# Gate and up products of a split-precision decoder turned token-major, with their results transposed for the down products and two of eight weight blocks used twice from one buffer

## The chip, the cores and the metric

The kernel runs on one core of a Trainium2 chip. A core has five engines that run side by side, each with its own queue of instructions: TensorE (PE; its weight loads are shown as PEld), VectorE (DVE), ScalarE (ACT), GpSimd (POOL) and SyncE (SP), which here issues the transfers between the chip's main memory and the on-chip memory SBUF. TensorE writes its sums into PSUM, eight banks of 128 partitions x 512 float32. The metric is the device time of one execution in microseconds (us); lower is better.

## The reference

Two layers; each is a half-step feed-forward, a mixing block (three kinds of attention, gated) and a second half-step feed-forward, with an RMS norm before and after each of them. Everything is float32. What the change touches are the four feed-forwards.

```python
D_MODEL = 1024; SEQ = 512; DEPTH = 2
D_FF = ((8 * D_MODEL // 3 + 127) // 128) * 128        # 2816

def _swiglu(t, w_gate, w_up, w_down):
    return (jax.nn.silu(t @ w_gate) * (t @ w_up)) @ w_down

for l in range(DEPTH):
    f = _swiglu(_rmsnorm(h, ffn1_pre_g[l]), ffn1_w_gate[l], ffn1_w_up[l], ffn1_w_down[l])
    h = h + 0.5 * _rmsnorm(f, ffn1_post_g[l])
    u = _rmsnorm(h, mix_pre_g[l])
    ...
    f = _swiglu(_rmsnorm(h, ffn2_pre_g[l]), ffn2_w_gate[l], ffn2_w_up[l], ffn2_w_down[l])
    h = h + 0.5 * _rmsnorm(f, ffn2_post_g[l])
```

## The kernel before

**Precision.** A float32 operand is split into a high part, rounded to TensorE's fp32r type (a cast on ScalarE, line 179), and a low part, the rest (a subtraction on VectorE, line 180). A product takes three matmuls (`mm3`, lines 205 to 207): high x high, high x low, low x high.

**Tiling of a feed-forward.** Tokens are 512, model features 1024, hidden features 2816. Of the hidden features 2048 are taken in two chunks (`ci` = 0, 1) of 1024; the last 768 are done plainly, with 512-wide matmuls. A chunk's gate product, up product and down product are each a 2 x 2 block product done with seven block products instead of eight (Strassen's scheme in Winograd's form): the seven are numbered n = 0 to 6 and run in the order `ORDER = (0, 2, 1, 3, 4, 5, 6)` in gate and up groups; `TO[n]` says which quarter of the result (half of the tokens, half of the chunk's features) is finished with product n; `SUM[n]` says which of three pairs of PSUM banks it adds into. Products 0, 3, 5 and 6 add on into one pair, and the result is read out on the way after 3, 5 and 6.

**Gate and up groups** (`feature_product`, line 727). The left factor is a sum of blocks of the normalized input, with features on the partitions, split into a high and a low tile: 4 slices (k) of 128 x 256 tokens. The first four products of a feed-forward's first gate group have these sums made beside them by VectorE and ScalarE (`sums`, line 680; tiles `x..`, `uh..`, `ul..`); later groups use them again. The right factor is a sum or difference of blocks of the weights, 4 slices of 128 x 512. A matmul holds 128 x 128 of the weights stationary and streams 256 tokens, so that the result has features on partitions. For a gate group the result goes through silu into tiles `s` (tag `f`, four buffers); for an up group VectorE multiplies it by the gate tile and writes it to `hr` (`hidden_rows`), for n = 4 and 5 after adding the part read out earlier (lines 764, 766, 771). Down products take their left factor from `hr` (`first_factor`, line 789: sums and splits), keep 128 x 128 of it stationary and stream 512 columns of weights (`product`, line 809).

**Weights.** A block of a product comes as two units (`BlockUnit`, line 274), each 2 slices of 128 x 512 float32 (512 KB), fetched by one transfer into a buffer with tag `raw` (2 buffers) or `o` (8, of which 4 are for this while the hidden state is parked in main memory). Per group the blocks fetched are those in `BLOCKS`, one for each of the seven products, and an eighth at n = 2 into a tile that is kept (`Keep`: names `tg`, `tu`, `bt`), in which VectorE builds differences (line 315). Names: `raw_ga`, `wh_ga`, `wl_ga` are the raw, high and low tiles of gate weights of the feed-forward `a` of a layer; `u` stands for up, `d` for down, `c` for the second feed-forward.

**Order of work.** A planner (`Queue`, line 338) holds the jobs in the order of `PLAN` (line 1576): seven gate products of chunk 0, seven up products, the same for chunk 1, then down products between plain gate and up work. When a job starts, its units are split and those of the next jobs (`AHEAD = 4` units) too; each time a unit's raw buffer is given back, `fetch_ahead` (line 399) issues the next transfers as far as the buffer counts in `RINGS` allow. A scheduler then sets the order of the instructions on each engine by their dependencies and priorities, and can place a few matmuls of the next group ahead of the last product of a group. On each engine instructions run in that order.

Of the kernel before, what the change touches and what calls it, by code (L numbers as in the profile page):

```python
# [13 lines left out]
ALU = mybir.AluOpType  # L14
# [3 lines left out]
P = 128  # L18
# [4 lines left out]
def kernel(  # L23
# [38 lines left out]
    nc = tc.nc  # L62
    _, S, D = x.shape
# [3 lines left out]
    ND = D // P  # L67
# [7 lines left out]
    FC = 8  # L75
# [12 lines left out]
    ident = cst.tile([P, P], F32, name="ident")  # L88
# [20 lines left out]
    def pbank(tag, name):  # L109
        return ps.tile([P, S], F32, tag=tag, bufs=4, name=name)  # L110
# [92 lines left out]
    def mm3(pt, lh, ll, rh, rl, start, stop, free=False):  # L203

        nc.tensor.matmul(pt, lh, rh, start=start, stop=False, skip_group_check=free)  # L205
        nc.tensor.matmul(pt, lh, rl, start=False, stop=False, skip_group_check=free)  # L206
        nc.tensor.matmul(pt, ll, rh, start=False, stop=stop, skip_group_check=free)  # L207
# [21 lines left out]
    PE_US = 1 / 2370.0  # L229


    class Unit:
# [26 lines left out]
        def loaded(self):  # L259
            self.raw = None  # L260
            Q.took(self.place, -1)
            Q.fetch_ahead()
# [11 lines left out]
    class BlockUnit(Unit):  # L274
# [9 lines left out]
        def __init__(self, n, src, rows, k0, nk, ncol, keep, name, place="raw"):  # L284
            super().__init__(src, k0, nk, 0, ncol, name)
            self.n, self.rows, self.keep, self.fetched, self.place = n, rows, keep, False, place

        def waits(self):
            return not self.fetched
# [6 lines left out]
        def fetch(self):  # L296
            if self.fetched:
                return
            self.fetched = True
            if self.n == 2:  # L300
                tc.keep_in_program_order(self.block(self.keep.get(self.k0), (0, 1)))
            Q.took(self.place, 1)
            self.raw = stile([P, self.nk, self.ncol], self.place, "raw_" + self.name, F32)
            self.block(self.raw[:], self.BLOCKS[self.n])

        def load(self):
            if self.h is not None:
# [282 lines left out]
    def ffn(l, src, wg, wu, wd, dst, name, spare, parked, plan, aside=None):  # L590
# [133 lines left out]
                return [block(i, j, part) for part in range(2)]  # L724
            return st["u", n]

        def feature_product(ci, up, n, uns):

            nm = f"{name}{'gu'[up]}_{ci}_{n}"
            if n in (0, 1, 2):  # L730
                st["c", n] = [pbank("z" if n == 0 else "mm", f"pw{nm}_{e}") for e in range(2)]
            if n == 1:
                for e in range(2):
                    nc.scalar.copy(st["c", 1][e][:], st["c", 0][e][:])
            if n == 0:
                if not up:
                    st["s", ci] = {}
            pts = st["c", SUM[n]]
            h, l = in_product(n)
            opens, ends = n in (0, 2), n in (1, 4, 6)  # L740
            for un in uns:
                for k in range(un.nk):
                    kk = un.k0 + k
                    for f in range(FC // 2):
                        c = slice(f * P, (f + 1) * P)
                        o = pts[f // 2][:, (f % 2) * S // 2:(f % 2 + 1) * S // 2]
                        mm3(o, un.h[:, k, c], un.l[:, k, c], h[:, kk], l[:, kk], opens and kk == 0 and f % 2 == 0,
                            ends and kk == FC // 2 - 1, free=True)
                        yield 3 * (S // 2) * PE_US
            if n == 0:  # L750
                return
            q = TO[n]
            g = st["s", ci]
            if not up and q not in g:
                g[q] = stile([P, FC // 2, S // 2], "f", f"s{name}_{ci}_{q[0]}{q[1]}", F32)[:]
            g = g[q]
            r = hidden_rows(2 * ci + q[1])[:, :, HALVES[q[0]]] if up else g
            for e in range(2):
                p = pts[e][:].rearrange("p (f q) -> p f q", f=2)
                re, ge = r[:, 2 * e:2 * e + 2], g[:, 2 * e:2 * e + 2]  # L760
                if n in (2, 3):
                    nc.scalar.copy(re, p)
                elif n in (4, 5):
                    nc.vector.tensor_tensor(re, re, p, ALU.add)
                elif up:
                    nc.vector.tensor_tensor(re, p, ge, ALU.mult)
                else:
                    nc.scalar.activation(re, p, AF.Silu)
            if n in (4, 5):
                if up:  # L770
                    nc.vector.tensor_tensor(r, r, g, ALU.mult)
                else:
                    nc.scalar.activation(r, r, AF.Silu)

        def feature_products(ci, up):

            w, nm = (wu if up else wg)[l, :, ci * FC * P:(ci + 1) * FC * P], f"{'gu'[up]}{name}_{ci}"
            keep = Keep(lambda k0: stile([P, 2, S], "o", f"t{nm}_{k0}", F32)[:])
            places = itertools.cycle(("raw", "o", "o"))
            for n in ORDER:  # L780
                uns = [BlockUnit(n, w, ND // 2, k, 2, S, keep, f"{nm}_{n}_{k}", next(places)) for k in range(0, ND // 2, 2)]
                run = lambda n=n, uns=uns: feature_product(ci, up, n, uns)
                early = ci == 0 and not up and n in ORDER[:4]
                yield uns, (lambda run=run: beside(run(), itertools.islice(st["some"], 1), 2)) if early else run

# [23 lines left out]
        def product(ci, n, uns):  # L809
            if n == 0 and ci == 0:  # L810
                RINGS["o"] = 2
                dst.begin()
            if n < 6:
                first_factor(ci, n + 1)
            if n in (0, 1, 2):
                st["b", SUM[n]] = [pbank("z", f"pd{name}_{ci}_{n}_{e}") for e in range(2)]
            pts = st["b", SUM[n]]
            if n == 1 and ci:
                for e in range(2):
                    nc.scalar.copy(pts[e][:], dst.fs[e][:, HF[0]])  # L820
            h, l = st["a", ci, n]
            opens, ends = n in (0, 2) or (n == 1 and not ci), n in (1, 4, 6)
            for un in uns:
                for k in range(un.nk):
                    kk = un.k0 + k
                    for e in range(2):
                        c = slice(e * P, (e + 1) * P)
                        mm3(pts[e][:], h[:, kk, c], l[:, kk, c], un.h[:, k], un.l[:, k], opens and kk == 0,
                            ends and kk == FC // 2 - 1, free=True)
                        yield 3 * S * PE_US  # L830
            if n == 0:
                return
            i, hf = TO[n]
            for e in range(2):
                f = dst.fs[2 * i + e][:, HF[hf]]
                if n == 1:
                    nc.scalar.copy(f, st["b", 0][e][:])
                    nc.vector.tensor_tensor(f, f, pts[e][:], ALU.add)
                elif ci == 0 and n in (2, 3, 6):
                    nc.scalar.copy(f, pts[e][:])  # L840
                else:
                    nc.vector.tensor_tensor(f, f, pts[e][:], ALU.add)

        def products(ci):

            keep = Keep(lambda k0: stile([P, 2, S], "o", f"bt{name}_{ci}_{k0}", F32)[:])
            w = wd[l, ci * FC * P:(ci + 1) * FC * P]
            for n in range(7):
                uns = [BlockUnit(n, w, FC // 2, k, 2, S, keep, f"d{name}_{ci}_{n}_{k}", ("raw", "o")[k // 2])
                       for k in range(0, FC // 2, 2)]  # L850
                yield uns, (lambda n=n, uns=uns: product(ci, n, uns))

        marks, made = {}, {}
# [16 lines left out]
        def queue(what):  # L870
            kind, n = what[0], what[1]
            if kind in "gu":
                if n not in made:
                    made[n] = plain(n)
                ms = (what[2],) if what[-1] in (0, 1) and len(what) == 3 else range(2)
                uns = made[n][kind == "u"]
                run = (lambda: gates(n, uns, ms)) if kind == "g" else (lambda: ups(n, uns, ms))
                Q.add(uns if ms[0] == 0 else [], run)
            elif kind == "a":
                Q.add([], lambda: iter(first_factor(n, 0) or ()))  # L880
            elif kind == "m":
                if name == "a0":
                    Q.add([], mem_stats)
            else:
                if what not in made:
                    made[what] = products(n) if kind == "d" else feature_products(n, kind == "U")
                for one in made[what]:
                    Q.add(*one)
                    break
# [746 lines left out]
```

## Time and profile before

| | |
|---|---|
| median of 3 runs | 2410.04 us (2409.96 to 2410.2) |
| profiled execution, whole | 2413.01 us |
| its span, first to last instruction | 2411.3 us |
| TensorE busy | 2383.9 us |
| VectorE busy | 1865.6 us |
| ScalarE busy | 1357.8 us |
| moved by transfers | 372.10 MB, mean 154 GB/s |

In profile rows, an instruction group has its line in the kernel, engine, operation, output <- inputs, shape and count. Rows of the timeline begin with the start and the duration in us. Matmuls are pipelined, so their durations overlap: the distance between two starts says what one costs in a stream, and the duration how long it is under way. In a row of waits stand who waited for what, and then the total in us, the times and the longest. In a row of the kind "270/272/273" stand the shortest, median and longest duration in ns, then the first and the last start.

### The profile page before, as it was taken

To read this page: it belongs to the slowest core of one execution; us is meant where nothing else is said; L and a number is where in the kernel's file an instruction comes from. 1 tells how busy PE (TensorE), PEld (TensorE's weight loads), DVE (VectorE), ACT (ScalarE), POOL (GpSimd) and SP (SyncE) were. 2 spreads that over 40 slices of the span, in tenths; PEclk is the share of its full clock that TensorE was granted. 3 is DMA by queue.
4 is the path that set the end of the run, shared out by engine and by line. 5 is a ranking of instruction groups with operands and counts; after the bars stand their busy time and mean duration, and the time that the engine had idled before them with its cause. 6 is when DMAs were issued, how large, how long until landed. Compare 5 with 4: busy or idle time off the path is not lost.

```text
span 2411.3 us, 36506 instructions
## 1 busy us (share of the span) xinstructions
PE 2383.9 (99%) x14407; PEld 2129.1 (88%) x14407; DVE 1865.6 (77%) x2462; ACT 1357.8 (56%) x2137; POOL 81.5 (3%) x134
## 2 busy tenths in 40 slices
PE   9999999999999999999999999999999999999998
PEld 8998889888888899988899988889888888999887
DVE  8878877678776688788698788766778766887885
ACT  6555565567655555455554554656676655545554
POOL 1000000000110000000000000000001100000000
PEclk9999999999999999999999999999999999999999
DMA  6765454222223466655557655542222234676544
GB/s 236 229 198 185 157 193 140 79 71 71 82 68 114 149 217 201 209 174 176 186 183 227 202 184 174 189 118 71 71 88 74 63 127 150 200 230 198 176 156 157
DMA packets 249344, 372.10 MB, mean 154 GB/s; under 512 B 11450, under 2 KB 126162, under 8 KB 249172
## 3 DMA queue, kind: packets, MB, share of 16 engines
q1 hardware_dynamic: 249076, 369.74, 47.9%
q8 instruction: 113, 1.85, 0.3%
q14 instruction: 59, 0.48, 0.1%
q0 software_dynamic: 96, 0.03, 0.0%
HBM read 357.14 MB, written 12.58 MB: 153 GB/s over the span
## 4 chain that ended last, share of the span: by engine, by line
PE 84%; DVE 7%; DMA 4%; ACT 3%; issue 2%; SPq 0%; DVEq 0%; ACTq 0%
PE pg L205 3%; PE pg L206 3%; PE pg L207 3%; PE pda L206 3%; PE pda L207 3%; PE pda L205 3%; PE pdc L206 2%; PE pdc L207 2%; PE pdc L205 2%; PE pb L207 1%; PE pb L206 1%; PE pb L205 1%; DMA raw_wo<-in_w_out_dram 1%; PE pwc1g L205 1%; PE pwc0g L205 1%
## 5 line engine op out<-in xcount | busy, mean ns | idle before, releaser
L205 PE MATMUL pg<-us_a,wh_wg 128*128 128x512 f32 x384 | 151.7, 395 | 0.0
L206 PE MATMUL pg<-us_a,wh_wg 128*128 128x512 f32 x384 | 150.6, 392 | 0.0
L207 PE MATMUL pg<-us_a,wl_wg 128*128 128x512 f32 x384 | 150.5, 392 | 0.0
L206 PE MATMUL pda<-wl_da,aha 128*128 128x512 f32 x224 | 87.5, 391 | 0.7 <-DVE wl_da L180 0.7
L206 PE MATMUL pdc<-wl_dc,ahc 128*128 128x512 f32 x224 | 87.5, 391 | 0.5 <-DVE wl_dc L180 0.5
L207 PE MATMUL pdc<-wh_dc,alc 128*128 128x512 f32 x224 | 87.2, 389 | 0.0
L207 PE MATMUL pda<-wh_da,ala 128*128 128x512 f32 x224 | 87.2, 389 | 0.0
L180 DVE TENSOR_TENSOR wl_dc<-raw_dc,wh_dc 128x1024 fp32r<-128x1024 f32 x50 | 61.1, 1222 | 33.2 <-ACT wh_dc L179 32.6
L205 PE MATMUL pda<-wh_da,aha 128*128 128x512 f32 x224 | 86.5, 389 | 0.0
L205 PE MATMUL pdc<-wh_dc,ahc 128*128 128x512 f32 x224 | 86.5, 389 | 0.0
L207 PEld LDWEIGHTS pg<-us_a,wl_wg 128*128 128x128 f32 x384 | 72.7, 189 | 15.5
L205 PEld LDWEIGHTS pg<-us_a,wh_wg 128*128 128x128 f32 x384 | 73.0, 190 | 14.6
L206 PEld LDWEIGHTS pg<-us_a,wh_wg 128*128 128x128 f32 x384 | 72.9, 190 | 14.6
L179 ACT CAST wh_dc<-raw_dc 128x1024 fp32r<-128x1024 f32 x50 | 52.7, 1053 | 57.6 <-PE pdc L207 17.7
L183 DVE SCALAR_TENSOR_TENSOR wl_wg<-raw_wg,wh_wg 128x1024 fp32r<-128x1024 f32 x48 | 58.5, 1223 | 33.9 <-ACT wh_wg L182 33.6
L180 DVE TENSOR_TENSOR wl_da<-raw_da,wh_da 128x1024 fp32r<-128x1024 f32 x50 | 61.1, 1222 | 24.4 <-ACT wh_da L179 23.9
L179 ACT CAST wh_da<-raw_da 128x1024 fp32r<-128x1024 f32 x50 | 52.6, 1053 | 44.4 <-PE pda L207 17.6
L179 ACT CAST wh_uc<-raw_uc 128x1024 fp32r<-128x1024 f32 x44 | 46.2, 1049 | 51.0 <-PE pwc0u L206 12.6
L180 DVE TENSOR_TENSOR wl_uc<-raw_uc,wh_uc 128x1024 fp32r<-128x1024 f32 x44 | 53.8, 1222 | 25.6 <-ACT wh_uc L179 24.9
L179 ACT CAST wh_ua<-raw_ua 128x1024 fp32r<-128x1024 f32 x44 | 46.0, 1049 | 41.6 <-PE pwa1u L206 12.6
L180 DVE TENSOR_TENSOR wl_ua<-raw_ua,wh_ua 128x1024 fp32r<-128x1024 f32 x44 | 53.6, 1221 | 20.0 <-ACT wh_ua L179 19.3
L182 ACT ACTIVATE wh_wg<-raw_wg 128x1024 fp32r<-128x1024 f32 x48 | 50.8, 1061 | 26.6 <-PE pv L1044 13.5
(640 smaller groups left out, 8933.2 us busy)
## 6 DMA issues: line engine op xcount, KB each, us to landing
raw_da<-in_ffn_w_down_dram SPq DMA_DIRECT2D x74, 512.0 KB, 4.7
raw_dc<-in_ffn_w_down_dram SPq DMA_DIRECT2D x74, 512.0 KB, 4.8
raw_ga<-in_ffn_w_gate_dram SPq DMA_DIRECT2D x68, 512.0 KB, 4.5
raw_ua<-in_ffn_w_up_dram SPq DMA_DIRECT2D x68, 512.0 KB, 4.3
raw_gc<-in_ffn_w_gate_dram SPq DMA_DIRECT2D x68, 512.0 KB, 4.2
raw_uc<-in_ffn_w_up_dram SPq DMA_DIRECT2D x68, 512.0 KB, 4.3
raw_wg<-in_w_gate_dram SPq DMA_DIRECT2D x48, 512.0 KB, 3.5
raw_wo<-in_w_out_dram SPq DMA_DIRECT2D x24, 512.0 KB, 3.7
```

The costliest lines, as they stand in the source:

```text
L179: both = [nc.scalar.copy(h_ap, src)]
L180: make = lambda: nc.vector.tensor_tensor(l_ap, src, h_ap.bitcast(F32), ALU.subtract)
L182: both = [nc.scalar.activation(h_ap, src, AF.Copy, scale=scale)]
L183: make = lambda: nc.vector.scalar_tensor_tensor(l_ap, src, scale, h_ap.bitcast(F32), ALU.mult, ALU.subtract)
L205: nc.tensor.matmul(pt, lh, rh, start=start, stop=False, skip_group_check=free)
L206: nc.tensor.matmul(pt, lh, rl, start=False, stop=False, skip_group_check=free)
L207: nc.tensor.matmul(pt, ll, rh, start=False, stop=stop, skip_group_check=free)
```

## The change

Gate and up products swap the roles of their factors: 128 x 128 of the activations are stationary, and 512 weight columns stream, so that the result has tokens on partitions. The product of silu(gate) and up is written over the gate tile; `turn` then transposes each finished quarter on TensorE, eight 128 x 128 transposes into two PSUM banks, and copies them on ScalarE into `hr`, where the down products find features on partitions as before. `turn` is called in the next product, after its third slice of four; for the last up product of chunk 1 this is the first down product.

Where two products that follow each other use the same block (n = 0 and 2, n = 3 and 4 in gate and up groups; n = 3 and 4 in down groups), the second takes over the buffer of the first (`inherits`) and issues no transfer; the buffer is given back after the second.

```diff
@@ class BlockUnit
             self.n, self.rows, self.keep, self.fetched, self.place = n, rows, keep, False, place
+            self.heir = None
+
+        def inherits(self, un):
+            un.heir, self.place = self, None
@@ fetch
             self.fetched = True
             if self.n == 2:
                 tc.keep_in_program_order(self.block(self.keep.get(self.k0), (0, 1)))
+            if self.place is None:
+                return
             Q.took(self.place, 1)
             self.raw = stile([P, self.nk, self.ncol], self.place, "raw_" + self.name, F32)
             self.block(self.raw[:], self.BLOCKS[self.n])
+
+        def loaded(self):
+            if self.heir is None:
+                super().loaded()
+            else:
+                self.heir.raw, self.heir.place, self.raw = self.raw, self.place, None
@@ feature_product, now token_product
-                    for f in range(FC // 2):
-                        c = slice(f * P, (f + 1) * P)
-                        o = pts[f // 2][:, (f % 2) * S // 2:(f % 2 + 1) * S // 2]
-                        mm3(o, un.h[:, k, c], un.l[:, k, c], h[:, kk], l[:, kk], opens and kk == 0 and f % 2 == 0,
-                            ends and kk == FC // 2 - 1, free=True)
-                        yield 3 * (S // 2) * PE_US
+                    for e in range(2):
+                        c = slice(e * P, (e + 1) * P)
+                        mm3(pts[e][:], h[:, kk, c], l[:, kk, c], un.h[:, k], un.l[:, k], opens and kk == 0,
+                            ends and kk == ND // 2 - 1, free=True)
+                        yield 3 * S * PE_US
+                    if kk == ND // 2 - 2:
+                        yield from turn("z")
...
                 elif up:
-                    nc.vector.tensor_tensor(re, p, ge, ALU.mult)
+                    nc.vector.tensor_tensor(ge, p, ge, ALU.mult)
...
             if n in (4, 5):
                 if up:
-                    nc.vector.tensor_tensor(r, r, g, ALU.mult)
+                    nc.vector.tensor_tensor(g, r, g, ALU.mult)
                 else:
                     nc.scalar.activation(r, r, AF.Silu)
-
-        def feature_products(ci, up):
+            if up and n in (1, 4, 5, 6):
+                st["turn"] = (f"{nm}", g, r)
+
+        def turn(tag):
+
+            nm, g, r = st.pop("turn", (None, None, None))
+            if nm is None:
+                return
+            g = g.rearrange("p f q -> p (f q)")
+            for b in range(2):
+                pt = pbank(tag, f"ht{nm}_{b}")
+                for f in range(2):
+                    for e in range(2):
+                        nc.tensor.transpose(pt[:, (2 * f + e) * P:(2 * f + e + 1) * P],
+                                            g[:, e * S + (2 * b + f) * P:][:, :P], ident[:])
+                nc.scalar.copy(r[:, 2 * b:2 * b + 2], pt[:].rearrange("p (f q) -> p f q", f=2))
+                yield 0.4
+
+        def token_products(ci, up):
...
-            places = itertools.cycle(("raw", "o", "o"))
+            places, had = itertools.cycle(("raw", "o", "o")), {}
             for n in ORDER:
-                uns = [BlockUnit(n, w, ND // 2, k, 2, S, keep, f"{nm}_{n}_{k}", next(places)) for k in range(0, ND // 2, 2)]
-                run = lambda n=n, uns=uns: feature_product(ci, up, n, uns)
+                uns = [BlockUnit(n, w, ND // 2, k, 2, S, keep, f"{nm}_{n}_{k}", n in (2, 4) or next(places))
+                       for k in range(0, ND // 2, 2)]
+                if n in (2, 4):
+                    for un, of in zip(uns, had[n - 2 + (n == 4)]):
+                        un.inherits(of)
+                had[n] = uns
+                run = lambda n=n, uns=uns: token_product(ci, up, n, uns)
@@ product (down)
                         yield 3 * S * PE_US
+                    if kk == FC // 2 - 2:
+                        yield from turn("mm")
@@ products (down)
+                if n == 4:
+                    for un, of in zip(uns, had):
+                        un.inherits(of)
+                had = uns
```

More of the change, by code (lines that the diff above doesn't have):

```diff
@@ L725, in in_product, with token_product @@
             return st["u", n]
-        def feature_product(ci, up, n, uns):
+        def token_product(ci, up, n, uns):
             nm = f"{name}{'gu'[up]}_{ci}_{n}"
@@ L885, in queue @@
                 if what not in made:
-                    made[what] = products(n) if kind == "d" else feature_products(n, kind == "U")
+                    made[what] = products(n) if kind == "d" else token_products(n, kind == "U")
                 for one in made[what]:
```

## The prediction

> **What bounds the kernel now.** I read the page's busy times first, then the same times by stage, then what the matmul engine waited for.
>
> ```profile
> span 2411.3 us, 36506 instructions
> PE 2383.9 (99%) x14407; PEld 2129.1 (88%) x14407; DVE 1865.6 (77%) x2462; ACT 1357.8 (56%) x2137; POOL 81.5 (3%) x134
> ...
> 38.80:82.00 43.20, 43.09 (x358) 42.75 (x357) 41.83 (x43) 28.09 (x35) 3.99 (x5) 1.00 0.65 209
> 82.00:122.50 40.50, 39.93 (x331) 39.53 (x330) 33.56 (x39) 23.89 (x29) 0.00 (x0) 1.00 0.70 213
> 122.50:163.00 40.50, 40.42 (x337) 40.22 (x336) 29.41 (x28) 22.58 (x27) 0.00 (x0) 1.00 0.67 209
> 163.00:204.00 41.00, 41.00 (x336) 40.59 (x336) 33.52 (x32) 21.53 (x25) 0.00 (x0) 1.00 0.39 116
> ```
>
> The last four rows are the gate, up, gate, up groups of the first feed-forward (length, then PE, PEld, DVE, ACT, POOL, clock, DMA share, GB/s). TensorE is busy all through at the full granted clock, so each group is paid in matmul time. The one engine near it is VectorE, above all in the first gate group (41.83 of 43.20 us). DMA is at 0.4 to 0.7. TensorE's waits in the whole run that lie in the stages touched:
>
> ```profile
> PE pdc L206 <- DVE wl_dc L180: 1.3, 2, 0.8
> PE pwa1g L207 <- DVE wl_ga L180: 1.2, 1, 1.2
> ...
> PE pda L206 <- DVE wl_da L180: 0.7, 1, 0.7
> PE pwc0g L207 <- DVE wl_gc L180: 0.7, 1, 0.7
> ...
> PE pwa0g L207 <- DVE wl_ga L180: 0.4, 1, 0.4
> ...
> PE pwc0u L205 <- DVE hrc L764: 0.2, 1, 0.2
> PE pwa0u L205 <- DVE hra L764: 0.2, 1, 0.2
> PE pwa1u L205 <- DVE hra L764: 0.2, 1, 0.2
> PE pwc1u L205 <- DVE hrc L764: 0.2, 1, 0.2
> ```
>
> That is 3.1 us in gate and up groups and 2.0 us in down products. Almost nothing can be won by ending waits; what counts is the time that the matmuls themselves take.
>
> **Part 1: half as many matmuls, each twice as wide.** Four feed-forwards x two chunks x gate and up are 16 groups of seven products. A product falls from 4 k x 4 f x 3 = 48 matmuls of 256 columns to 4 k x 2 e x 3 = 24 of 512: 5,376 become 2,688, with as many weight loads fewer. Their durations (0.28 and 0.39 us below) overlap, so the price is the distance between starts, in stretches without a wait:
>
> ```profile
> 180.10 0.28 PE L207 MATMUL pwa0u<-uha,wl_ua 128*128 128x256 f32 x1
> ...
> 189.82 0.28 PE L207 MATMUL pwa0u<-uha,wl_ua 128*128 128x256 f32 x1
> ...
> 228.90 0.39 PE L207 MATMUL pda<-wh_da,ala 128*128 128x512 f32 x1
> ...
> 235.70 0.39 PE L207 MATMUL pga<-us_x,wl_ga 128*128 128x512 f32 x1
> ```
>
> The first pair lies 81 matmuls apart: 9.72/81 = 120.0 ns. The second lies 30 apart: 6.80/30 = 226.7 ns. The down products (pda) already have the new shape: a 128x128 piece of activations stationary, 512 weight columns moving. Two narrow ones cost 240.0, one wide one 226.7: 13.3 ns saved, x 2,688 = **-35.8 us**, 0.32 us a product.
>
> The Trainium skill, page "TensorE: Matmul & The Clock Gate", section "Back-to-back issue gap", gives a gap of N/2.4 + 2.5 ns for a matmul of N columns at full clock, so only 2.5 ns per instruction. By it the saving would be an estimated 6.7 us and the whole change slower. The rows speak against it here: 120.0 and 226.7 fit 256 and 512 columns at 2.4 per ns plus 13.3 ns each.
>
> **Part 2: transposes.** The result now has tokens on partitions, and the down products want features there. Each up group transposes four tiles (`turn`), each with 8 transposes and 2 ScalarE copies: 32 turns, 256 transposes, 64 copies. The same operation, eight at a time between wide matmuls, stands in the trace:
>
> ```profile
> 1554.29 0.39 PE L207 MATMUL pda<-wh_da,hida 128*128 128x512 f32 x1
> 1554.53 1.03 PE L565 MATMUL uta<-ident,fa 128*128 128x128 f32 x8
> ...
> 1555.63 0.40 PE L206 MATMUL pda<-wl_da,hida 128*128 128x512 f32 x1
> ...
> L565 PE MATMUL uta<-ident,fa x64: 270/272/273, 356.6 to 1575.1; 128*128 128x128 f32 x64
> ...
> 698.88 0.39 PE L205 MATMUL pq<-us_a,wh_q 128*128 128x512 f32 x1
> 699.28 1.28 PE L1081 MATMUL ptf<-ident,pf 128*128 128x128 f32 x10
> ...
> 700.63 0.40 PE L207 MATMUL pq<-us_a,wl_q 128*128 128x512 f32 x1
> ```
>
> From 1554.29 to 1555.63 is 1.34 us with two wide matmuls in it: 1.34 - 0.45 = 0.88 us for eight or 0.89 us for eight, restart included. 32 x 0.88 = **+28.2 us**. The attention row bounds it from above: 1.75 - 0.45 = 1.30 for ten, waits included, 33 us in all. The price is on the path, since TensorE has no gaps to hide it in.
>
> The same page, section "Part 4: PE-mode transpose", reports about 275 ns for a transpose inside a kernel. The 270/272/273 agrees as the duration of one, but eight take 0.88 us, so most of it overlaps; 256 x 0.272 would be 70 us.
>
> The copies are new work for ScalarE. Nearest row, the same size out of PSUM:
>
> ```profile
> L762 ACT COPY hra<-pwa0u x8: 567/584/591, 92.8 to 185.9; 128x512 f32<-128x512 f32 x8
> ```
>
> 64 x 0.58 = 37 us, 4.7 us in an up group where ScalarE works 21.5 to 23.9 of 41 us: hidden. Uncovered it would be 37 us. A copy waits for its transposes, and behind it on ScalarE wait the casts of the weights two products ahead; they have about a product to spare.
>
> **Part 3: do the transposes wait?** They stand after 18 of 24 matmuls of the next product, 18 x 0.2267 = 4.1 us after the product that they belong to. The multiply must be done by then, or all that TensorE has queued waits. The trace gives the lateness of that chain twice, after the fifth product (n=4) of an up group:
>
> ```profile
> 106.84 1.23 DVE L315 TENSOR_TENSOR tga<-tga,raw_ga 128x1024 f32<-128x1024 f32 x1 [1.62 <-DMA raw_ga<-in_ffn_w_gate_dram]
> ...
> 109.12 0.68 DVE L764 TENSOR_TENSOR hra<-hra,pwa0u 128x512 f32<-128x512 f32 x1
> ...
> 112.70 1.22 DVE L771 TENSOR_TENSOR hra<-hra,sa 128x1024 f32<-128x1024 f32 x1
> ...
> 114.36 0.28 PE L205 MATMUL pwa0g<-us_x,wh_ga 128*128 128x256 f32 x1
> ...
> 190.14 1.41 DVE L764 TENSOR_TENSOR hra<-hra,pwa0u 128x512 f32<-128x512 f32 x2
> 191.58 1.22 DVE L771 TENSOR_TENSOR hra<-hra,sa 128x1024 f32<-128x1024 f32 x1
> ...
> 196.42 0.39 PE L205 MATMUL pda<-wh_da,aha 128*128 128x512 f32 x1
> ```
>
> In the first up group the sixth product ended at 114.36, so the fifth at 114.36 - 5.76 = 108.60; its multiply ended at 113.92, 5.3 us late. In the second the sixth ended at 196.42, the fifth at 190.66, its multiply at 192.80, 2.1 us late. The first was late because VectorE stood 1.62 us on a weight load and because splits lay between the three steps. In the changed program's instruction order the three stand together, and the step that waited (L315) uses a block that the group has loaded two places earlier in the queue. I take 2.1 us, hence no wait; bounds 0 and the 14 us of the second rival.
>
> **Part 4: loads kept.** Two blocks of eight per gate or up group and one of eight per down product are read from the buffer of the product before: 16 x 4 + 8 x 2 = 80 loads fewer. SyncE's instruction list confirms it (711 before, 631 after). TensorE waits for no load directly. The load that held VectorE at 106.84 in the first up group goes, and with it I expect the L207 rows above (0.4 + 0.7 + 1.2): **-2.3 us**, bounds 0 and -3.1. Buffers are held one product longer, but fewer are wanted. Of the 2.0 us in down products I take half: **-1.0 us**, bounds 0 and -2.0.
>
> **Part 5: VectorE becomes the limit in places.** It has the same work, in less time:
>
> ```profile
> 60.92 1.21 DVE L180 TENSOR_TENSOR ula<-x11a,uha 128x1024 fp32r<-128x1024 f32 x1
> ...
> 61.98 0.28 PE L205 MATMUL pwa0g<-uha,wh_ga 128*128 128x256 f32 x1
> 62.18 0.39 PE L206 MATMUL pwa0g<-ula,wh_ga 128*128 128x256 f32 x1
> ...
> 911.73 1.22 DVE L180 TENSOR_TENSOR ulc<-x11c,uhc 128x1024 fp32r<-128x1024 f32 x1
> ...
> 914.05 0.28 PE L205 MATMUL pwc0g<-uhc,wh_gc 128*128 128x256 f32 x1
> ```
>
> In the first gate group the operand of the fifth product is ready at 62.13, when it is wanted. After the change the product starts 4 x 0.32 = 1.28 us sooner, at 60.70, and wants it at its third matmul, 61.15; the new order puts one more VectorE step (1.14 us) ahead of it, 63.27: **+2.1 us**. In the second feed-forward it is ready at 912.95 and would be wanted at 914.05 - 1.28 + 0.45 = 913.22: no wait, and I take the other two to be alike. At worst all four first gate groups lose their whole 7 x 0.32 = 2.24 us: 9 us; at best 0.
>
> The seventh product adds into banks that VectorE must first have read. The last matmul on the first bank starts four places before the sixth product's end (-0.91 us) and lasts 0.39, the read takes 0.68 (L764): 0.16 us too late, with signalling about 0.3. Gate groups cover this with matmuls of the next group put in front; in the eight up groups nothing is put in front any more: 8 x 0.3 = **+2.4 us**, bounds 0 and 4.
>
> **Sum:** -35.8 + 28.2 - 2.3 - 1.0 + 2.1 + 2.4 = **-6.4 us**. The profiled execution took 2413.0 us (span 2411.3 and 1.7 around it) and would take 2406.6; the runs shown have their median 3.0 lower, so I forecast 2410.0 - 6.4 = **2403.6**. (0.2%, about what a measurement can tell from no change, is 4.8 us.)
>
> **Rivals.**
> - *Even.* VectorE swallows the gate groups' saving in all four first groups: 9.0 in place of 2.1, so +0.5, 2410.5. For it: 41.83 of 43.20 us. Against: the 1.1 us to spare at 911.73.
> - *Slower: the transposes wait.* The place is the fifth and seventh product's multiply. If every up group is as late as the first was (5.3 us, and 0.5 us beyond 4.1 on the seventh), each loses 1.2 + 0.5 = 1.7, eight lose 14: -6.4 + 14 = +7.6, 2417.6. It decides from 4.1 us of lateness; the second up group shows 2.1.
> - *Slower: matmul time goes by columns alone.* Then 512 columns cost twice 120.0, nothing is saved, and 2403.6 + 35.8 = 2439. The skill's 2.5 ns (section named above) points this way. Against: 226.7 in the trace for the same shape.
> - *Slower: transposes at their full duration.* +70 in place of 28: 2445. The skill's 275 ns (section named above) could be read this way. Against: eight in 0.88 us.
> - That loads are not dropped after all is ruled out by the count of 80.
>
> **How the numbers follow.** Forecast 0.50, even 0.33, waiting transposes 0.12, columns 0.02, full-length transposes 0.03. Faster by over 0.2%: 0.50; within: 0.33; slower: 0.17. With all bounds favourable -35.8 + 27.8 - 3.1 - 2.0 = -13, 2397; the even case with bounds of +4 and dearer transposes reaches 2414. The range 2398 to 2414 leaves out the last three cases. The forecast's own is 2398 to 2407.
>
> **What would show it.** Up-group matmuls 0.227 us apart, eight transposes in about 0.88 us, no TensorE wait on the multiply (lines 779 and 784 of the changed kernel) before them; a wait of some 2 us at the fifth product of the first gate group; the L207 waits gone; VectorE's share up, the weight-load engine's down. It is wrong if wide matmuls in these groups start more than 0.23 us apart, if a turn takes over 1.1 us, or if TensorE's waits in the gate and up groups add up to more than 12 us.

## The result and the profile after

The changed kernel took 2400.98 us (median of 5, 2398.38 to 2401.47) beside 2409.96 us of the kernel before (2407.76 to 2410.20): ratio 0.9960, 95% interval 0.9950 to 0.9971, 9.0 us less. The forecast was 6.4 us less, 2403.6, with a range of 2398 to 2414. The spans of the two profiled executions differ by more, 12.1 us; the last section shows a part of why.

The page's busy times of the changed kernel (engine, us, share, instructions):

```profile
span 2399.2 us, 31431 instructions
PE 2375.6 (99%) x11975; PEld 2012.0 (84%) x11975; DVE 1867.4 (78%) x2462; ACT 1393.9 (58%) x2201; POOL 81.5 (3%) x134
```

There are 2,432 fewer matmul records (2,688 fewer matmuls and 256 transposes more) and 117 us less of weight loads; VectorE is busy as long as before (1865.6 us then), and ScalarE 36 us longer, with the 64 copies. TensorE stays the bound. The timeline of the second up group, with a turn (eight transposes) in it:

```profile
179.78 1.03 PE L800 MATMUL hta0u<-ident,sa 128*128 128x128 f32 x8
180.57 0.48 PE L205 MATMUL pwa0u<-wh_ua,uha 128*128 128x512 f32 x1
...
188.83 0.39 PE L205 MATMUL pwa0u<-wh_ua,uha 128*128 128x512 f32 x1
...
191.32 0.39 PE L207 MATMUL pwa0u<-wh_ua,ula 128*128 128x512 f32 x1
191.55 1.03 PE L800 MATMUL hta0u<-ident,sa 128*128 128x128 f32 x8
192.34 0.48 PE L205 MATMUL pwa0u<-wh_ua,uha 128*128 128x512 f32 x1
192.66 0.40 PE L206 MATMUL pwa0u<-wl_ua,uha 128*128 128x512 f32 x1
...
193.57 0.39 PE L207 MATMUL pwa0u<-wh_ua,ula 128*128 128x512 f32 x1
194.15 0.47 PE L205 MATMUL pwa0u<-wh_ua,us_x 128*128 128x512 f32 x1 [0.19 <-DVE hra L777]
194.46 0.39 PE L206 MATMUL pwa0u<-wl_ua,us_x 128*128 128x512 f32 x1
```

From 188.83 to 191.32 are 11 matmuls: 226.4 ns each. From 191.32 to 192.66 is 1.34 us with two matmuls of 0.227 in it: 0.89 us for a turn, the last 0.09 of it paid by the matmul behind it (0.32 to the next start). Added up over all 32 turns in the trace, it is 28.3 us. At 194.15 stands the change from the sixth to the seventh product: it starts 0.58 us after the start before, so 0.35 late, and the next matmul is 0.08 later still. What TensorE waited for, now (total, times, longest):

```profile
PE pwa0g L207 <- DVE ula L180: 1.1, 1, 1.1
...
PE pda L206 <- DVE wl_da L180: 0.6, 2, 0.4
...
PE pwc0u L205 <- DVE hrc L777: 0.4, 2, 0.2
PE pwc1u L205 <- DVE hrc L777: 0.4, 2, 0.2
PE pwa1u L205 <- DVE hra L777: 0.4, 2, 0.2
PE pwa0u L205 <- DVE hra L777: 0.4, 2, 0.2
```

The L207 waits on gate weights (`wl_ga`, `wl_gc`) and the waits on `wl_dc` are gone. The wait for `ula` in the first gate group is new. The wait for VectorE's read of the bank ahead of the seventh product (L777, the L764 of the kernel before) now stands in all eight up groups; before it stood in four. No row names the transposes' inputs (L779, L784). How near they came to being late, VectorE and TensorE show in the second up group:

```profile
193.93 1.22 DVE L833 TENSOR_TENSOR asa<-hra,hra 128x1024 f32<-128x1024 f32 x1
195.13 1.22 DVE L180 TENSOR_TENSOR wl_da<-raw_da,wh_da 128x1024 fp32r<-128x1024 f32 x1
...
197.80 1.22 DVE L784 TENSOR_TENSOR sa<-hra,sa 128x1024 f32<-128x1024 f32 x1
...
199.18 1.04 PE L800 MATMUL hta0u<-ident,sa 128*128 128x128 f32 x8
```

A sum and a split for the down products go first, so the sixth product's multiply ends at 199.02, 5.1 us after that product, and the turn begins 0.16 us later. It stands after 21 matmuls of the seventh product, not 18: the scheduler moved it by three in all four up groups of second chunks. By an estimate (three matmuls of 0.227 us, less the 0.16 to 0.19 us to spare) it would have waited about 0.5 us in each after 18.

### The profile page after: what moved, and what is told of

It is laid out like the page before. It is cut to its first block, busy times and chain, and to the rows that moved or that the text cites. A ratio compares the mean times of both kernels' runs of the same rounds, so it can differ in the third digit from the quotient of the medians.

```text
span 2399.2 us, 31431 instructions
## 1 busy us (share of the span) xinstructions
PE 2375.6 (99%) x11975; PEld 2012.0 (84%) x11975; DVE 1867.4 (78%) x2462; ACT 1393.9 (58%) x2201; POOL 81.5 (3%) x134
## 4 chain that ended last, share of the span: by engine, by line
PE 86%; DVE 7%; ACT 3%; DMA 2%; issue 1%; SPq 0%; POOL 0%; DVEq 0%; ACTq 0%
PE pg L205 3%; PE pg L206 3%; PE pg L207 3%; PE pda L206 3%; PE pda L207 3%; PE pda L205 3%; PE pdc L206 3%; PE pdc L207 3%; PE pdc L205 3%; PE pb L207 2%; PE pb L206 2%; PE pb L205 2%; PE pwo L207 1%; PE pwo L205 1%; PE pwo L206 1%
## 5 line engine op out<-in xcount | busy, mean ns | idle before, releaser
L205 PE MATMUL pg<-us_a,wh_wg 128*128 128x512 f32 x384 | 151.2, 394 | 0.0
L206 PE MATMUL pg<-us_a,wh_wg 128*128 128x512 f32 x384 | 150.6, 392 | 0.0
L207 PE MATMUL pg<-us_a,wl_wg 128*128 128x512 f32 x384 | 150.3, 391 | 0.0
L206 PE MATMUL pda<-wl_da,aha 128*128 128x512 f32 x224 | 87.7, 392 | 0.6 <-DVE wl_da L180 0.6
L206 PE MATMUL pdc<-wl_dc,ahc 128*128 128x512 f32 x224 | 87.7, 392 | 0.0
L205 PE MATMUL pdc<-wh_dc,ahc 128*128 128x512 f32 x224 | 87.5, 391 | 0.0
L205 PE MATMUL pda<-wh_da,aha 128*128 128x512 f32 x224 | 87.5, 390 | 0.0
L207 PE MATMUL pda<-wh_da,ala 128*128 128x512 f32 x224 | 87.4, 390 | 0.0
L207 PE MATMUL pdc<-wh_dc,alc 128*128 128x512 f32 x224 | 87.3, 390 | 0.0
L207 PEld LDWEIGHTS pg<-us_a,wl_wg 128*128 128x128 f32 x384 | 72.6, 189 | 15.4
L206 PEld LDWEIGHTS pg<-us_a,wh_wg 128*128 128x128 f32 x384 | 72.6, 189 | 14.4
L205 PEld LDWEIGHTS pg<-us_a,wh_wg 128*128 128x128 f32 x384 | 72.5, 189 | 14.5
L1353 POOL CAST k<-k 64x1024 fp32r<-64x1024 f32 x16 | 18.5, 1154 | 1335.3 <-DVE k L180 1309.2
```

The costliest lines, as they stand in the source:

```text
L1353: nc.gpsimd.tensor_copy(t[ro, j::2], t[r, j::2])
```

## The experiments

Medians in us; the ratio is to the kernel before, run beside it on the same chip. The first four share one chip, the next four another, the last four a third.

| run | median | before | ratio (95%) |
|---|---|---|---|
| changed_again | 2400.14 | 2409.13 | 0.9964 (0.9952 to 0.9977) |
| fetch_all | 2408.20 | 2409.13 | 0.9996 (0.9988 to 1.0005) |
| feature_keep | 2403.23 | 2409.13 | 0.9977 (0.9968 to 0.9985) |
| turn_before_seventh | 2397.17 | 2409.13 | 0.9952 (0.9939 to 0.9966) |
| half_width | 2440.75 | 2410.21 | 1.0130 (1.0115 to 1.0146) |
| no_transposes | 2374.02 | 2410.21 | 0.9850 (0.9837 to 0.9864) |
| turn_after_first_slice | 2404.57 | 2410.21 | 0.9978 (0.9969 to 0.9986) |
| seventh_and_pool | 2401.07 | 2410.21 | 0.9964 (0.9952 to 0.9977) |
| fetch_gate_up | 2408.18 | 2410.63 | 0.9991 (0.9982 to 0.9999) |
| fetch_down | 2399.35 | 2410.63 | 0.9959 (0.9946 to 0.9973) |
| seventh_again | 2394.36 | 2410.63 | 0.9936 (0.9924 to 0.9949) |
| seventh_and_order | 2395.30 | 2410.63 | 0.9935 (0.9923 to 0.9948) |

**The two halves of the change, each alone.** The changed kernel itself:

> The changed kernel once more, beside the three below, so that they are compared on one chip. It took 2401.0 us against 2410.0 of before, 9.0 less. If that difference is the kernel's own it comes again within 2 us. If the 3 us by which the profiled execution of before lay above its median (2413.0 against 2410.0) were the rule on another chip, the difference is up to 12.

The difference came again: 9.0 us. Now without the kept loads:

```diff
-                uns = [BlockUnit(..., n in (2, 4) or next(places)) ...]
-                if n in (2, 4):
-                    for un, of in zip(uns, had[n - 2 + (n == 4)]):
-                        un.inherits(of)
+                uns = [BlockUnit(..., next(places)) ...]
...
-                if n == 4:
-                    for un, of in zip(uns, had):
-                        un.inherits(of)
```

> Undoes part 4 alone: token-major products and transposes as in the changed kernel, but every product fetches its own blocks, 80 loads more. Theory: the kept loads took the L207 waits of the first up groups and part of the waits in the down products away (2.3 + 1.0 us in the prediction; by the distances between starts in the two traces up to 5.0 + 2.5), so without them this takes 3 to 7 us more than the changed kernel, 2404 to 2408, with VectorE standing on a load and TensorE waiting behind it in the first up groups. Rival: the new order of the instructions (the add and the multiply together, no matmuls of the next group put in front in up groups) ended these waits, and the kept loads are worth nothing: 2401, within 1 us of the changed kernel.

And the kept loads on the kernel before, its feature-major products untouched:

```diff
-            places = itertools.cycle(("raw", "o", "o"))
+            places, had = itertools.cycle(("raw", "o", "o")), {}
...
+                if n in (2, 4):
+                    for un, of in zip(uns, had[n - 2 + (n == 4)]):
+                        un.inherits(of)
```

> Part 4 alone on the kernel before: feature-major products as before, no transposes, but the two blocks of eight (one in down products) are kept and used twice, 80 loads fewer. Theory (kept loads end the waits): 3 to 7 us less than before, 2403 to 2407, and the L207 waits of the first up groups (0.4, 1.2, 0.7 us) gone. Rival (the new order ended them): 2410, within 1 us of before, and the L207 waits still there.

The four combinations, on one chip: before 2409.1, kept loads alone 2403.2 (-5.9), token-major alone 2408.2 (-0.9, within the noise), both 2400.1 (-9.0). In both runs the time came as the theory had it, and the rival fell: the kept loads are worth 5.9 us in the kernel before and 8.1 in the token-major one. In `fetch_all` it is not the L207 waits that come back, but others:

```profile
PE hta0u L800 <- DVE sa L784: 2.1, 1, 2.1
...
PE htc0u L800 <- DVE sc L784: 0.7, 1, 0.7
PE htc1u L800 <- DVE sc L784: 0.7, 1, 0.7
PE hta1u L800 <- DVE sa L784: 0.7, 1, 0.7
```

There the transposes do wait, for the fifth product's multiply in the four up groups of first chunks, at a place that the prediction's slower rival named. By the distances between starts these four waits cost 4.9 us. VectorE in the first up group of `fetch_all`, then in the changed kernel's:

```profile
106.58 1.23 DVE L327 TENSOR_TENSOR tga<-tga,raw_ga 128x1024 f32<-128x1024 f32 x1 [2.64 <-DMA raw_ga<-in_ffn_w_gate_dram]
...
112.33 1.22 DVE L784 TENSOR_TENSOR sa<-hra,sa 128x1024 f32<-128x1024 f32 x1
```

```profile
102.09 1.23 DVE L327 TENSOR_TENSOR tga<-tga,raw_ga 128x1024 f32<-128x1024 f32 x1 [2.21 <-DMA tga<-in_ffn_w_gate_dram]
...
109.49 1.23 DVE L784 TENSOR_TENSOR sa<-hra,sa 128x1024 f32<-128x1024 f32 x1
```

VectorE stands on a load in both (2.64 and 2.21 us). But where a block is kept, the next group's blocks are asked for earlier: SyncE issues the load that VectorE stands on at 102.1 us in `fetch_all` and at 97.6 in the changed kernel, and each lands 4.4 us later. So this load is not faster, but earlier. The subtraction runs 4.5 us sooner, and the multiply ends 2.8 us sooner, before its transposes. In `feature_keep` the list of waits has no L207 row:

```profile
PE utx L1549 <- DVE fx L1558: 1.6, 1, 1.6
PE warm L1519 <- DVE warm L1611: 1.3, 1, 1.3
PE pda L206 <- DVE wl_da L180: 1.1, 1, 1.1
PE pdc L206 <- DVE wl_dc L180: 1.0, 1, 1.0
```

**Which loads.** The first edit above, alone, then the second:

> The changed kernel with its gate and up groups fetching all blocks again (64 loads more), down products still keeping theirs. In the trace of the kernel that fetched everything, 7.4 us more than in the changed kernel stand in the up groups: 4.9 in waits of the transposes (2.1 and three times 0.7 at the fifth quarter's multiply), 2.5 in waits for splits. Theory: all of the 8 us by which that kernel was slower come from here: 8 us more than the changed kernel, 2408, with the same waits in the list. Rival (the loads of down products share in it through the queue): 2403 to 2406, and the rest in the next run.

> The changed kernel with its down products fetching all blocks again (16 loads more), gate and up groups still keeping theirs. Theory (all of it lies in the up groups): within 1 us of the changed kernel, 2400. By the prediction's step it is 1.0 us, 2401; its bound is 2.0, 2402, with waits on the splits of down weights in the list.

Fetching in gate and up groups costs what fetching everything did (ratio 0.9991 beside 0.9996; the transposes wait again, 2.3, 1.0, 0.8 and 0.5 us, and splits and casts of up weights 0.9 and 0.6). Fetching in down products costs nothing that can be seen (0.9959). The theory held; the prediction's 1.0 us for down products did not come from the loads.

**What a matmul costs.** Each wide matmul cut in two:

```diff
-                        mm3(pts[e][:], h[:, kk, c], l[:, kk, c], un.h[:, k], un.l[:, k], ...)
+                        for x in range(2):
+                            w = slice(x * S // 2, (x + 1) * S // 2)
+                            mm3(pts[e][:, w], h[:, kk, c], l[:, kk, c], un.h[:, k, w], un.l[:, k, w], ...)
```

> The changed kernel with each 512-wide matmul of gate and up groups cut in two of 256 columns with the same stationary piece: 2,688 become 5,376 again, everything else (token-major, transposes, kept loads) stays. Theory of the forecast: a matmul costs its columns and 13.3 ns (120.0 and 226.7 ns between starts), so 2,688 x 13.3 = 35.8 us more than the changed kernel's 2400.1, less up to 2 us because the first gate group then no longer waits for VectorE: 2434 to 2436. Rival: the 13.3 ns belong to changing the stationary piece and not to the instruction, so two halves with one piece cost little: under 2408. By the rule of 2.5 ns an instruction (the Trainium skill, page TensorE: Matmul & The Clock Gate, section Back-to-back issue gap) it would be an estimated 6.7 us, 2407.

It took 30.5 us more than before, so some 39.5 more than the changed kernel: more than the theory, and far from the times of the rivals. In its second up group:

```profile
179.79 0.28 PE L206 MATMUL pwa0u<-wl_ua,us_x 128*128 128x256 f32 x1
...
180.75 0.28 PE L205 MATMUL pwa0u<-wh_ua,us_x 128*128 128x256 f32 x1
```

Eight matmuls in 0.96 us are 120 ns each, with tokens stationary as with weights. Its gate and up groups are 32 us longer in the trace (35.8 less 3.8 of waits). The other 7.6 us stand under `pdc`, in down products that the edit does not touch: TensorE waits 4.0 us for `wl_dc` and 3.0 for `fc` (none and 1.3 in the changed kernel), and a half-speed stretch follows the longest wait for `wl_dc` (2.3). Why VectorE is later there stays open.

The run leaves one rival of its own untested. Each half still loads its stationary piece (14,663 matmuls and 14,663 weight loads in its trace), so two halves behind one load, which that rival speaks of, were not run. The trace shows that it does not matter whether the piece changes: L205 and L206 use the same one, L207 another, and all steps are 120 ns. Whether the 13.3 ns belong to the matmul or to the load that goes with it stays open.

**What the transposes cost.** They are left out, and ScalarE copies from the gate tile as it lies, so this kernel's result is another:

```diff
-                pt = pbank(tag, f"ht{nm}_{b}")
-                for f in range(2):
-                    for e in range(2):
-                        nc.tensor.transpose(...)
-                nc.scalar.copy(r[:, 2 * b:2 * b + 2], pt[:].rearrange(...))
+                nc.scalar.copy(r[:, 2 * b:2 * b + 2], g[:, b * S:(b + 1) * S].rearrange(...))
```

> The changed kernel without the 256 transposes: ScalarE copies the gate tile as it lies into the tile that the down products read (64 copies of the same size, from SBUF in place of PSUM), so the values are not turned and the output is another. Theory: the transposes lie wholly on the path, 32 x 0.885 = 28.3 us: 2371.8. Rival: they give VectorE and the loads time that is needed anyway, and without them TensorE waits in the up groups: 2375 to 2385, with waits on VectorE's splits in the list.

It took 36.2 us less than before, so some 27 less than the changed kernel: the theory's 28.3 less about 1, the rival in small. The transposes' time is on the path, and a little of it had hidden these waits, both on gate matmuls that the scheduler put into the first up group (in the profiled execution 7 matmuls at half pace follow, 1.4 us):

```profile
PE pwa0g L205 <- ACT wh_ga L179: 1.3, 1, 1.3
...
PE pwa0g L206 <- DVE wl_ga L180: 0.8, 1, 0.8
```

**Where the transposes stand.** Earlier:

```diff
-                    if kk == ND // 2 - 2:
+                    if kk == 0:
                         yield from turn("z")
```

> The changed kernel with the transposes asked for after the first of four slices of the next product in place of the third; in the order on TensorE they then stand after 6 to 10 matmuls for most turns, not after 18. Theory (the multiplies are late by 1.7 to 5 us, and the place after 18 matmuls is what hides it): in the changed kernel's trace the multiply is done 0.2 to 3.2 us before its transposes start; moved forward by 8 to 12 matmuls of 0.227 us, the first up group's first two turns miss it by about 2.1 and 1.4 us, the other turns by 0 to 0.3, in all 5 to 8 us: 2405 to 2408, with TensorE's waits on lines 779 and 784 in the list. Rival (there is room enough, the place does not matter): within 1 us of 2400.1.

The turns now stand after 6, 10 and 9 matmuls, and in second chunks the sixth product's after 18. It took 5.6 us less than before where the changed kernel takes 9.0 less: 3.4 are lost, a little under the theory's 5 to 8, and outside the rival's 1. Two kinds of wait grew:

```profile
PE hta0u L800 <- DVE sa L779: 1.7, 2, 1.4
...
PE pwa0u L205 <- DVE hra L777: 0.8, 2, 0.4
PE pwc0u L205 <- DVE hrc L777: 0.8, 2, 0.4
```

Only the first turn of the first up group waits (1.4 and 0.3 us); no row names L784. The wait for the read of the bank ahead of the seventh product is twice what it was; the theory did not have it. Then one turn is put where TensorE waits anyway:

```diff
-                    if kk == ND // 2 - 2:
+                    if kk == ND // 2 - 2 and n != 5:
                         yield from turn("z")
+            if n == 5:
+                yield from turn("z")
```

> The changed kernel with one of the four turns of each up group put elsewhere: the transposes of the fifth product's quarter stand between the sixth and the seventh product in place of after 18 matmuls of the sixth. In the changed kernel's trace the seventh product's first matmul starts 0.35 us late in all eight up groups, and the second 0.08, because VectorE has not read the bank yet. Theory: that wait is one for the read alone, and 0.88 us of transposes lie over it: 8 x 0.43 = 3.4 us less than the changed kernel, 2397.5. Rival: the transposes' banks or the copies that they now push back (the casts of the weights wait behind these on ScalarE) cost as much again: 2401 or more, with TensorE's waits on the weights' casts or splits in the seventh product.

> The kernel with the fifth quarter's transposes ahead of the seventh product once more, beside the next one: 2397.2 before, so 2396 to 2398, 3 us under the changed kernel, and no wait on the read of the bank in up groups.

On the first chip it took 2397.2 beside the changed kernel's 2400.1, near the 3.4 us of the theory, and 12.0 less than before; on the third 2394.4, 16.3 less than before. Why the same kernel gains 4 us more there is not shown, but both times it is faster than before and than the changed kernel (`fetch_down`, level with it, took 2399.4 on the third chip). The L777 rows are gone from its list; in the first up group the seventh product now starts behind the transposes:

```profile
112.19 1.03 PE L802 MATMUL hta0u<-ident,sa 128*128 128x128 f32 x8
113.44 0.47 PE L205 MATMUL pwa0u<-wh_ua,us_x 128*128 128x512 f32 x1 [0.22 <-ACT wh_ga L179]
```

**The wait of the first gate group.** On top of that kernel, one subtraction moved off VectorE:

```diff
-            tt(x11, x11, x21, ALU.subtract)
+            nc.gpsimd.tensor_tensor(x11, x11, x21, ALU.subtract)
```

> The kernel with the fifth quarter's transposes ahead of the seventh product (2397.2), and in each feed-forward's first gate group one of the sums that VectorE makes beside it (the subtraction for the sixth product's factor, 1.14 us in VectorE's stream) given to GpSimd, which is idle there. In the changed kernel the fifth product of the first feed-forward's gate group waits 1.8 us for VectorE, and no other first gate group does. Theory: VectorE's work alone is what is late, so the split comes two places (2.3 us) sooner in its order and the wait goes: 1.1 to 1.8 us less, 2395.4 to 2396.1. Rival: GpSimd slows VectorE while both run, or its own subtraction is late for the sixth product: 2397 or more, with the wait on the sixth product's operand.

The rival's time was right, 2401.1, 9.1 less than before: all that the seventh product's turn had won is lost. The wait did not move to the sixth product, as the rival had it. It grew at the fifth, from 1.1 to 1.6 us, and the fifth product of the three other first gate groups now waits 0.5 us each, as do three up groups behind them. From the timeline:

```profile
48.20 3.35 POOL L718 TENSOR_TENSOR x00a<-x00a,x10a 128x1024 f32<-128x1024 f32 x1
...
49.22 3.41 DVE L180 TENSOR_TENSOR ula<-x11a,uha 128x1024 fp32r<-128x1024 f32 x1
52.56 1.21 DVE L327 TENSOR_TENSOR tga<-raw_ga,tga 128x1024 f32<-128x1024 f32 x1
```

VectorE's step beside GpSimd's took 3.41 us, not 1.21. It lost 2.2 us, about what the two places (2.3 us) were to win. The same aim without GpSimd:

```diff
             yield "S2"
-            tt(x11, x11, x21, ALU.subtract)
...
             pair(4, s)
+            tt(x11, x11, x21, ALU.subtract)
             yield "S4"
```

> The same, and in each feed-forward's first gate group the subtraction for the sixth product's factor stands after the fifth product's factor in place of before it, on VectorE: the same instructions, in an order in which the fifth product's split comes two places (2.3 us) sooner and the sixth's also two. (Given to GpSimd, that subtraction took 3.35 us there and the VectorE step beside it 3.41 in place of 1.21, so nothing was won.) Theory: the 1.8 us that the first gate group loses at its fifth product go, 1.3 to 1.8 us under the kernel ahead of it, 2395.4 to 2395.9. Rival: VectorE is full there, and the wait only comes at a later product of that group: the same as the kernel ahead of it, 2397.

There is no difference (0.9935 beside 0.9936). VectorE's lateness shows later, as the rival had it, though not in that gate group but at the start of the first up group:

```profile
73.50 0.50 PE L206 MATMUL pwa0u<-wl_ua,us_x 128*128 128x512 f32 x1 [1.37 <-DVE wl_ua L180]
```

Two orders have one sum: VectorE is full there (in the changed kernel it is busy 42.07 of the 42.40 us from 39.00 to 81.40).

## Why the prediction was right, point by point

- **Part 1, -35.8 us.** Shown: 226 ns in place of two times 120 in the groups themselves, and 120 again when they are cut. The rival "by columns alone" falls, and so does the rule of 2.5 ns for this stream. The section that gives it (the Trainium skill, page "TensorE: Matmul & The Clock Gate", section "Back-to-back issue gap") says that it is the gap of an isolated matmul and that in a stream the weight load sets the spacing too; the prediction did not say so.
- **Part 2, +28.2 us.** Shown: 28.3 in the trace, 27 when the transposes are left out. The copies are hidden: no row of TensorE's waits names them (L802). The full-length rival falls.
- **Part 3, no waits.** Right for the changed kernel, in part by luck. That the load on which VectorE stood would come sooner was a good reason: without the kept loads the slower rival's wait is there, 2.1 us and three times 0.7. The other reason fails: the 2.1 us of lateness were read from one multiply, and the sixth product's in second chunks are 5 us late. That the place after 21 matmuls saves these is an estimate.
- **Part 4, -3.3 us: the term that was mis-sized.** Measured are -5.9 alone and -8.1 with token-major products, both beyond its bounds (-3.1 and -2.0, in all -5.1). The step that failed was to take the rows of the list of waits (0.4 + 0.7 + 1.2) as the price. The kernel before, third feed-forward:

```profile
1313.21 0.28 PE L206 MATMUL pwa1g<-us_c,wh_ga 128*128 128x256 f32 x1
1314.68 0.38 PE L207 MATMUL pwa1g<-us_c,wl_ga 128*128 128x256 f32 x1 [1.19 <-DVE wl_ga L180]
1315.28 0.38 PE L205 MATMUL pwa1u<-us_c,wh_ua 128*128 128x256 f32 x1 [0.21 <-DVE hra L764]
```

The row says 1.2; the starts say 1.47 and 0.60 where 0.12 each is due, 1.83 lost. Added up over the gate and up groups in this way, 6.8 us are lost in the kernel before and 1.7 in `feature_keep`: 5.1 of its 5.9. In the token-major kernel the loads prevent other losses, 7.4 us by the same count in `fetch_all` beside the changed kernel: the 4.9 of the transposes' waits and 2.5 at splits and the matmuls behind them. The prediction named the load in Part 3 and Part 4, but had a price for these waits in neither. The -1.0 for down products is not theirs.
- **Part 5, +2.1 and +2.4 us.** The first gate group lost 1.8 at its fifth product, the others nothing, as forecast. The bank read cost 0.43 in each of eight up groups, 3.5 in all, where 0.3 was forecast.
- **The sum.** In gate and up groups with their transposes the trace shows -6.6 us (matmuls with the waits between them 651.9 to 620.0, transposes 25.3; the 3.0 that are missing from 28.3 are paid by the matmuls behind). The prediction's terms for these groups make -5.4. They come so near in part by luck: waits and late starts in these groups go from 6.8 to about 8 us, where the prediction had 2.3 go and 4.5 come. The kept loads' term was too small, and so was the bank reads'. The other 5.5 us between the two spans lie elsewhere: the output projection 89.1 to 87.5 us, down products 442.1 to 440.0, the gates of the mixing block (`pg`) 269.8 to 268.5, and smaller ones. By the medians, 9.0 us apart, some 2.4 lie there. The loads of the down products are not the cause (`fetch_down`); what is was not tried.

## What to carry to other kernels

Price a wait by the distance between starts around it, not by its row: the restart and the next wait that it causes belong to it. When two edits come together, measure all four combinations: here the layout alone gains nothing sure, the kept loads alone 5.9 us, both 9.0, because the loads keep VectorE early enough for the layout's transposes. Work that must be on TensorE anyway is best put where it waits for a bank.

## What the runs showed of the hardware that was not expected

**Half-speed stretches.** In some profiles TensorE runs some 3 us at half pace shortly after a wait. In `fetch_all`, behind a wait of 2.2 us, matmuls of 512 columns start 0.427 us apart, and the granted clock of the stage (after POOL's column) is 0.51:

```profile
1200.00:1207.80 7.80, 5.62 (x33) 4.58 (x32) 5.47 (x9) 4.57 (x9) 0.00 (x0) 0.98 0.64 188
1207.80:1211.00 3.20, 3.20 (x9) 2.50 (x8) 2.98 (x7) 0.68 (x3) 0.00 (x0) 0.51 0.83 264
```

Each such matmul costs 0.2 us more, so a stretch of 5 to 7 costs 1 to 1.4 us. The profiled execution of before has two (11 such matmuls), the changed kernel's one (7), `turn_before_seventh` none: that is 0.8 of the 12.1 us between the spans. In `seventh_and_pool` one follows a wait of 1.6 us; the wait of 2.6 us for `fc` in the kernel before has none. The Trainium skill, page "TensorE: Matmul & The Clock Gate", section "What's actually happening", has the clock fall to half after an idle window of about 3.4 us; here half-speed stretches followed shorter waits, though not each time, and what decides it was not tried.

**GpSimd holds VectorE up.** The 3.41 us above: VectorE's step ended 1.1 us after GpSimd's, as if it had begun only then. In the three other feed-forwards the step beside GpSimd's took 3.42 to 3.43 us and also ended 1.1 us after it. The Trainium skill, page "SBUF — State Buffer", section "SBUF: two separate sides", says that a VectorE instruction with two SBUF inputs and a GpSimd instruction that reads SBUF lock each other out for the whole instruction; the trace agrees.
